# A load of 28 rows split in 26 and 2, and an early store that waits for the landing of the 26

## The chip, the cores and the metric

The kernel runs on one core of a Trainium2 chip. The metric is the time of one execution on the device in microseconds (us). A second execution of the same program is recorded by the hardware profiler; its span runs from the first to the last instruction of the program.

## The reference

There are 16 x 1024 = 16384 tokens, each with 512 float32 values in `x` and 8 router logits. For each token the two largest probabilities of the softmax over the 8 logits are taken and divided by their sum. The output holds the token's 512 values twice, once multiplied by each of the two weights:

```python
probs = np.exp(router_logits - logits_max)
probs = probs / np.sum(probs, axis=-1, keepdims=True)
topk_indices = np.argsort(probs, axis=-1)[..., -k:]          # k = 2
topk_probs = np.take_along_axis(probs, topk_indices, axis=-1)
topk_probs = topk_probs / np.sum(topk_probs, axis=-1, keepdims=True)
x_expanded = x[:, :, np.newaxis, :].repeat(k, axis=2)
return (x_expanded * topk_probs[..., np.newaxis]).astype(np.float32)
```

By the profile the kernel reads 34.08 MB from HBM and writes 67.11 MB.

## The kernel before

The tokens are laid over the 128 partitions, 128 for each partition, in two groups (`GROUPS`): 65 tokens a partition, then 63. In what follows a "row" is one token of each partition: a row of input is 128 x 2 KB = 256 KB, a row of output 512 KB. Tokens of one partition lie side by side in HBM, so that a load or store of n rows moves one contiguous piece a partition.

There are two large buffers. `xs` has room for 65 rows of input. `osp` has room for 18 rows of output; before that it serves as room for the logits and for the steps that find the two largest (`room`). The output of a row is either written into `osp` or, where the input rows have been used up, over input rows in `xs` itself (two rows of `xs` hold one row of output).

**Loads** (`LOADS`, the loop of line 119, issued at line 122). The first group comes in four loads of 2, 4, 28 and 31 rows, the second in three of 16, 16 and 31. All are issued by SyncE, in the order in which they are written. Behind the first 6 rows stand the two loads of the logits (lines 130 and 131), and `top2_weights` is built there: VectorE finds the largest and the second of the 8 logits by maxima and minima, and ScalarE makes the two weights from their difference by two sigmoids (lines 37 and 38), into `WA`.

**Products and stores** (`STORES`, the loop of line 134). One entry is the first row, the number of rows, the buffer, and the place in it. For each entry VectorE makes one product (line 138) of the input rows, each read twice, by the weights; where it is written over a part of `osp` that an earlier store may still be reading, the product is made in two, so that the first rows (`FREE`: 3 and 2) don't wait for the second store to be done. Then the entry is stored (line 151). In the first group the entries are 3, 15, 16, 15 and 16 rows; in the second 16, 16, 15 and 16.

**Queues.** Every load and store is issued by SyncE, in the written order, save one: the first store of the first group, of 3 rows (the early store), which ScalarE issues behind its two sigmoids. The profile shows SyncE's DMAs as queue q1 and ScalarE's as q10. The instructions wait on semaphores for what they need, and SyncE's issues stand in a row: one that waits holds those behind it. The second group's loads are written over the rows of `xs` whose stores they wait for.

Of the kernel before, what the change touches and what calls it, by code (L numbers as in the profile page):

```python
# [1 line left out]

# [4 lines left out]

F32 = mybir.dt.float32
ALU = mybir.AluOpType
ACTF = mybir.ActivationFunctionType  # L10
P = 128


def top2_weights(nc, WA, dlt, room, logits, E):

    tt = nc.vector.tensor_tensor
    hi, lo, n = None, None, E  # L20
    while n > 1:
        n //= 2
        if hi is None:
            a, b = logits[:, :, 0:n], logits[:, :, n : 2 * n]
            nhi, nlo = room(n), b
            tt(nhi, a, b, op=ALU.max)  # L26
            tt(nlo, a, b, op=ALU.min)  # L27
        else:
            a, b = hi[:, :, 0:n], hi[:, :, n : 2 * n]
            nhi, nlo, tmp = room(n), room(n), room(n)  # L30
            tt(tmp, lo[:, :, 0:n], lo[:, :, n : 2 * n], op=ALU.max)  # L31
            tt(nlo, a, b, op=ALU.min)  # L32
            tt(nlo, nlo, tmp, op=ALU.max)  # L33
            tt(nhi, a, b, op=ALU.max)  # L34
        hi, lo = nhi, nlo
    tt(dlt, hi[:, :, 0], lo[:, :, 0], op=ALU.subtract)  # L36
    nc.scalar.activation(WA[:, :, 0], dlt, ACTF.Sigmoid, scale=-1.0)  # L37
    return nc.scalar.activation(WA[:, :, 1], dlt, ACTF.Sigmoid, scale=1.0)  # L38

GROUPS = [65, 63]

LOADS = [[2, 4, 28, 31], [16, 16, 31]]
BASE = [0, 1]

STORES = [
    [(0, 3, "osp", 0), (3, 15, "osp", 3), (18, 16, "xs", 0), (34, 15, "osp", 0), (49, 16, "xs", 33)],
    [(0, 16, "osp", 2), (16, 16, "xs", 0), (32, 15, "osp", 0), (47, 16, "xs", 32)],
]  # L50

L = 18

FREE = [3, 2]


@with_exitstack
def kernel(
    ctx: ExitStack,
    tc: tile.TileContext,  # L60
    x: bass.AP,
    router_logits: bass.AP,
    k: bass.AP,
    out: bass.AP,
):
    nc = tc.nc
    B, S, D = x.shape
    E = router_logits.shape[-1]
    N = B * S
    assert int(k) == 2 and E == 8 and N == P * sum(GROUPS)  # L70
    M = N // P

    x_v, o_v, rl_v = [], [], []
    t0 = 0
    for n in GROUPS:
        t1 = t0 + P * n
        x_v.append(
            x.rearrange("b s d -> (b s) d")[t0:t1].rearrange("(p m) d -> p m d", p=P)
        )
        o_v.append(  # L80
            out.rearrange("b s k d -> (b s) k d")[t0:t1].rearrange(
                "(p m) k d -> p m k d", p=P
            )
        )
        rl_v.append(
            router_logits.rearrange("b s e -> (b s) e")[t0:t1].rearrange(
                "(p m) e -> p m e", p=P
            )
        )
        t0 = t1  # L90

    wpool = ctx.enter_context(tc.tile_pool(name="wpool", bufs=1))
    xs = wpool.tile([P, max(GROUPS), D], F32)
    osp = wpool.tile([P, L, 2, D], F32)
    WA = wpool.tile([P, M, 2], F32)
    dlt = wpool.tile([P, M], F32)


    flat = osp.rearrange("p l k d -> p (l k d)")
    taken = [0]  # L100

    def room(n):
        o = taken[0]
        taken[0] += M * n
        return flat[:, o : o + M * n].rearrange("p (m n) -> p m n", n=n)

    logits = room(E)

    def place(where, at, n):

        if where == "osp":
            return osp[:, at : at + n]
        return xs[:, at : at + 2 * n, :].rearrange("p (r k) d -> p r k d", k=2)

    moved = []
    m0 = 0
    for g, G in enumerate(GROUPS):
        x0, r = BASE[g], 0
        for n in LOADS[g]:
            moved.append(  # L120
                tc.keep_in_program_order(
                    nc.sync.dma_start(  # L122
                        xs[:, x0 + r : x0 + r + n, :], x_v[g][:, r : r + n, :]
                    )
                )
            )
            r += n
            if g == 0 and r == 6:
                n0 = GROUPS[0]
                tc.keep_in_program_order(nc.sync.dma_start(logits[:, :n0], rl_v[0]))  # L130
                tc.keep_in_program_order(nc.sync.dma_start(logits[:, n0:], rl_v[1]))  # L131
                weights = top2_weights(nc, WA, dlt, room, logits, E)
        assert r == G
        for r, n, where, at in STORES[g]:
            og = place(where, at, n)
            again = where == "osp" and at == 0 and r > 0
            for a, b in [(0, FREE[g]), (FREE[g], n)] if again else [(0, n)]:
                product = nc.vector.tensor_tensor(  # L138
                    og[:, a:b],
                    xs[:, x0 + r + a : x0 + r + b, :]  # L140
                    .unsqueeze(2)
                    .to_broadcast([P, b - a, 2, D]),
                    WA[:, m0 + r + a : m0 + r + b, :]
                    .unsqueeze(3)
                    .to_broadcast([P, b - a, 2, D]),
                    op=ALU.mult,
                )

            queue = nc.scalar if g == r == 0 else nc.sync
            moved.append(  # L150
                tc.keep_in_program_order(queue.dma_start(o_v[g][:, r : r + n], og))  # L151
            )
        m0 += G

    seen = tc.keep_in_program_order(nc.sync.nop())
    for ins in [weights, product] + moved[:-1]:
        tc.add_manual_dep(
            seen.ins,
            ins.ins.name,
            mybir.DependencyInfo(  # L160
                mybir.DependencyClass.Sync, mybir.DependencyReason.DATA
            ),
            reason="all but the last transfer is done",
        )


# [1 line left out]
_INS = ['x', 'router_logits', 'k']  # L168
_OUTS = [((16, 1024, 2, 512), 'float32')]

_NUMBERS = {'k': 2}


# [26 lines left out]
```

## Time and profile before

| | |
|---|---|
| time, median of 3 runs | 239.78 us (239.72 to 239.96) |
| the profiled execution | 241.36 us |
| its span | 239.6 us |
| VectorE busy | 141.9 us, 59% of the span, 22 instructions |
| ScalarE busy | 1.8 us |
| read from HBM, written to HBM | 34.08 MB, 67.11 MB; 422 GB/s over the span |
| VectorE's longest waits | for loads of `xs` 47.3 us, 2 times; for stores of `osp` 14.8 us, 2 times |

A profile line that has a count like "x22" gives the number of instructions. SPq and ACTq are the instruction queues of SyncE and ScalarE, where DMAs are issued; the duration beside a DMA issue is that of the issue alone, and the time to its landing is told apart. Times in the timeline are from the start of the span. In windows, the DMA share is the time of all packets that start in the window, over 16 DMA engines; in a narrow window it can be over 1, since a packet is counted whole in the window where it starts.

### The profile page before, as it was taken

To read this page: it belongs to the slowest core of one execution; us is meant where nothing else is said; L and a number is where in the kernel's file an instruction comes from. 1 tells how busy PE (TensorE), PEld (TensorE's weight loads), DVE (VectorE), ACT (ScalarE), POOL (GpSimd) and SP (SyncE) were. 2 spreads that over 40 slices of the span, in tenths; PEclk is the share of its full clock that TensorE was granted. 3 is DMA by queue.
4 is the path that set the end of the run, shared out by engine and by line. 5 is a ranking of instruction groups with operands and counts; after the bars stand their busy time and mean duration, and the time that the engine had idled before them with its cause. 6 is when DMAs were issued, how large, how long until landed. Compare 5 with 4: busy or idle time off the path is not lost.

```text
span 239.6 us, 106 instructions
## 1 busy us (share of the span) xinstructions
DVE 141.9 (59%) x22; ACT 1.8 (1%) x3; POOL 0.2 (0%) x4
## 2 busy tenths in 40 slices
DVE  0560499999789999200000699999405999960000
ACT  2000000000000000000000000000000000000000
POOL 0000000000000000000000000000000000000000
DMA  7989998979989897999899999999999899898984
GB/s 253 528 373 483 427 415 376 493 339 492 481 372 492 383 482 339 482 437 449 361 421 438 438 438 498 435 419 471 405 405 471 372 503 442 380 492 360 514 350 186
DMA packets 2592, 101.19 MB, mean 422 GB/s; under 512 B 288, under 2 KB 416, under 8 KB 672
## 3 DMA queue, kind: packets, MB, share of 16 engines
q1 hardware_dynamic: 2448, 99.62, 96.7%
q10 hardware_dynamic: 144, 1.57, 1.5%
HBM read 34.08 MB, written 67.11 MB: 422 GB/s over the span
## 4 chain that ended last, share of the span: by engine, by line
DMA 48%; DVE 40%; SPq 1%; issue 0%; DVEq 0%
DMA xs<-in_x_dram 25%; DVE osp L138 25%; DMA out_dram<-osp 23%; DVE xs L138 14%; SPq L122 0%; SPq L131 0%; SPq L130 0%; SPq L151 0%; DVEq L138 0%
## 5 line engine op out<-in xcount | busy, mean ns | idle before, releaser
L138 DVE TENSOR_TENSOR osp<-xs,WA 128x3072 f32<-128x3072 f32 (+5 forms) x7 | 69.4, 9909 | 62.7 <-DMA xs<-in_x_dram 47.3
L138 DVE TENSOR_TENSOR xs<-xs,WA 128x16384 f32<-128x16384 f32 x4 | 68.9, 17224 | 0.1
L26 DVE TENSOR_TENSOR osp<-osp 128x512 f32<-128x512 f32 x1 | 0.7, 693 | 8.5 <-DMA osp<-in_router_logits_dram 8.5
L37 ACT ACT_TABLE_LOAD x1 | 1.3, 1283 | 0.7 <-PEq L181 0.7
L27 DVE TENSOR_TENSOR osp<-osp 128x512 f32<-128x512 f32 x1 | 0.7, 691 | 0.0
L32 DVE TENSOR_TENSOR osp<-osp 128x256 f32<-128x256 f32 (+1 forms) x2 | 0.7, 351 | 0.0
L31 DVE TENSOR_TENSOR osp<-osp 128x256 f32<-128x256 f32 (+1 forms) x2 | 0.7, 350 | 0.0
L34 DVE TENSOR_TENSOR osp<-osp 128x256 f32<-128x256 f32 (+1 forms) x2 | 0.7, 350 | 0.0
L33 DVE TENSOR_TENSOR osp<-osp 128x256 f32<-128x256 f32 (+1 forms) x2 | 0.7, 350 | 0.0
L37 ACT ACTIVATE WA<-dlt 128x128 f32<-128x128 f32 x1 | 0.3, 315 | 10.5 <-DVE dlt L36 10.5
L36 DVE TENSOR_TENSOR dlt<-osp 128x128 f32<-128x128 f32 x1 | 0.3, 292 | 0.0
L38 ACT ACTIVATE WA<-dlt 128x128 f32<-128x128 f32 x1 | 0.3, 297 | 0.0
L181 POOL MEMSET const-bfloat16-1.0<- 128x1 bf16 x1 | 0.1, 101 | 0.0
L181 POOL MEMSET const-uint8-127<- 128x1 uint8 x1 | 0.1, 101 | 0.0
L181 POOL MEMSET const-float32-0.0<- 128x1 f32 x1 | 0.1, 98 | 0.2 <-issue 0.2
L181 POOL MEMSET const-float32-1.0<- 128x1 f32 x1 | 0.1, 98 | 0.0
## 6 DMA issues: line engine op xcount, KB each, us to landing
out_dram<-osp SPq DMA_DIRECT2D x3, 7680.0 KB, 23.5
xs<-in_x_dram SPq DMA_DIRECT2D x2, 7936.0 KB, 42.2
xs<-in_x_dram SPq DMA_DIRECT2D x2, 4096.0 KB, 40.1
xs<-in_x_dram SPq DMA_DIRECT2D x1, 7168.0 KB, 24.8
out_dram<-osp ACTq DMA_DIRECT2D x1, 1536.0 KB, 26.6
xs<-in_x_dram SPq DMA_DIRECT2D x1, 1024.0 KB, 5.9
xs<-in_x_dram SPq DMA_DIRECT2D x1, 512.0 KB, 3.9
osp<-in_router_logits_dram SPq DMA_DIRECT2D x1, 260.0 KB, 6.2
```

The source lines that it names most:

```text
L26: tt(nhi, a, b, op=ALU.max)
L27: tt(nlo, a, b, op=ALU.min)
L31: tt(tmp, lo[:, :, 0:n], lo[:, :, n : 2 * n], op=ALU.max)
L32: tt(nlo, a, b, op=ALU.min)
L33: tt(nlo, nlo, tmp, op=ALU.max)
L34: tt(nhi, a, b, op=ALU.max)
L36: tt(dlt, hi[:, :, 0], lo[:, :, 0], op=ALU.subtract)
L37: nc.scalar.activation(WA[:, :, 0], dlt, ACTF.Sigmoid, scale=-1.0)
L38: return nc.scalar.activation(WA[:, :, 1], dlt, ACTF.Sigmoid, scale=1.0)
L138: product = nc.vector.tensor_tensor(og[:, a:b], xs[:, x0 + r + a : x0 + r + b, :] .unsqueeze(2) .to_broadcast([P, b - a, 2, D]), WA[:, m0 ...
L181: nc = _bacc.Bacc("TRN2", target_bir_lowering=False, num_devices=1)
```

## The change

The first group's load of 28 rows is issued as two, of 26 rows and of 2 rows, one behind the other on SyncE; the load of 31 rows follows as before. The early store of three rows, on ScalarE, gets one more thing to wait for: the landing of the load of 26. The second product (rows 3 to 17) then reads rows of the loads of 4 and 26 alone, so that it waits for the load of 26, and the third (rows 18 to 33) waits for the load of 2 as well. The function that adds such waits, `behind`, is also used for the instruction at the end that waits for all but the last transfer, as the code before it did in place. The order of the instructions on every engine is otherwise the same.

```diff
-LOADS = [[2, 4, 28, 31], [16, 16, 31]]
+LOADS = [[2, 4, 26, 2, 31], [16, 16, 31]]
...
+    def behind(ins, others, reason):
+
+        for other in others:
+            tc.add_manual_dep(
+                ins.ins,
+                other.ins.name,
+                mybir.DependencyInfo(
+                    mybir.DependencyClass.Sync, mybir.DependencyReason.DATA
+                ),
+                reason=reason,
+            )
+
...
             r += n
+            if g == 0 and r == 32:
+                landed = moved[-1]
             if g == 0 and r == 6:
...
             queue = nc.scalar if g == r == 0 else nc.sync
-            moved.append(
-                tc.keep_in_program_order(queue.dma_start(o_v[g][:, r : r + n], og))
-            )
+            store = tc.keep_in_program_order(queue.dma_start(o_v[g][:, r : r + n], og))
+            if queue is nc.scalar:
+                behind(store, [landed], "the store goes beside the last load of the group")
+            moved.append(store)
...
     seen = tc.keep_in_program_order(nc.sync.nop())
-    for ins in [weights, product] + moved[:-1]:
-        tc.add_manual_dep(
...
+    behind(
+        seen, [weights, product] + moved[:-1], "all but the last transfer is done"
+    )
```

More of the change, by code (lines that the diff above doesn't have):

```diff
@@ L149 @@
             queue = nc.scalar if g == r == 0 else nc.sync
-            moved.append(
-                tc.keep_in_program_order(queue.dma_start(o_v[g][:, r : r + n], og))
-            )
+            store = tc.keep_in_program_order(queue.dma_start(o_v[g][:, r : r + n], og))
+            if queue is nc.scalar:
+                behind(store, [landed], "the store goes beside the last load of the group")
+            moved.append(store)
         m0 += G
     seen = tc.keep_in_program_order(nc.sync.nop())
-    for ins in [weights, product] + moved[:-1]:
-        tc.add_manual_dep(
[L158 to L164, printed above, removed]
+    behind(
+        seen, [weights, product] + moved[:-1], "all but the last transfer is done"
+    )
 _INS = ['x', 'router_logits', 'k']
```

## The prediction

> **What bounds the kernel now.** I read the page first: the busy shares, the slices and the queues.
>
> ```profile
> span 239.6 us, 106 instructions
> DVE 141.9 (59%) x22; ACT 1.8 (1%) x3; POOL 0.2 (0%) x4
> DMA  7989998979989897999899999999999899898984
> q1 hardware_dynamic: 2448, 99.62, 96.7%
> q10 hardware_dynamic: 144, 1.57, 1.5%
> ```
>
> VectorE works 59% of the span; the packets of the two DMA queues (q1 is SyncE's, q10 is ScalarE's, which carries the early store alone) fill 96.7 + 1.5 = 98.2% of what 16 DMA engines have. The page's chain of waits gives DVE 40% of the span, but a chain through an engine that was released by a DMA doesn't say that the DMA engines stood still meanwhile. So next the stretches: DMA share and GB/s are the last two columns.
>
> ```profile
> 2.00:44.00 42.00, 23.73 (x14) 0.52 (x3) 0.00 (x0) 1.00 1.02 430
> 44.00:124.00 80.00, 50.28 (x4) 0.00 (x0) 0.00 (x0) 1.00 1.00 432
> 124.00:160.00 36.00, 26.38 (x2) 0.00 (x0) 0.00 (x0) 1.00 1.00 431
> 160.00:236.00 76.00, 41.52 (x4) 0.00 (x0) 0.00 (x0) 1.00 1.00 434
> ```
>
> Here the share is 1.00 in every stretch (1.02 in the first, since a packet is counted whole where it starts). The DMA engines go from packet to packet without a hole from 2 to 236 us. The bytes don't change, so only two things can move the time: a hole that the change opens, or packets that take longer or shorter. All holes of before together (1.8% of 239.6 = 4.3 us) lie at the start, before the first packets, and at the end, and the change touches neither.
>
> **Does a hole open?** The timeline of the first group, and the landings of the loads of 7168 KB (28 rows) and 7936 KB (31 rows), issued between 3 and 4 us by the rows of their issues:
>
> ```profile
> 16.40 0.37 ACTq L151 DMA_DIRECT2D out_dram<-osp  x1
> 27.42 16.16 DVE L138 TENSOR_TENSOR osp<-xs,WA 128x15360 f32<-128x15360 f32 x1 [11.04 <-DMA xs<-in_x_dram]
> 43.60 0.35 SPq L151 DMA_DIRECT2D out_dram<-osp  x1
> 43.61 17.22 DVE L138 TENSOR_TENSOR xs<-xs,WA 128x16384 f32<-128x16384 f32 x1
> 60.75 3.35 DVE L138 TENSOR_TENSOR osp<-xs,WA 128x3072 f32<-128x3072 f32 x1
> 60.86 0.34 SPq L151 DMA_DIRECT2D out_dram<-xs  x1
> 67.08 12.96 DVE L138 TENSOR_TENSOR osp<-xs,WA 128x12288 f32<-128x12288 f32 x1 [2.98 <-DMA out_dram<-osp]
> 80.07 0.33 SPq L151 DMA_DIRECT2D out_dram<-osp  x1
> ...
> xs<-in_x_dram SPq DMA_DIRECT2D x1, 7936.0 KB, 45.6
> xs<-in_x_dram SPq DMA_DIRECT2D x1, 7168.0 KB, 24.8
> ...
> out_dram<-xs SPq DMA_DIRECT2D x1, 25.5
> ```
>
> The load of 28 lands at 27.4 (issue near 2.6 + 24.8), and the second product starts then. The load of 31 lands at about 3.3 + 45.6 = 48.9, the second store is issued at 43.60: it stands in the queue 5.3 us before its turn. The third store is issued at 60.86, while the second lands just before 67.08 (the product of 12 rows waits for it and starts then): 6.2 us early. The fourth is issued at 80.07 and the third lands at 60.86 + 25.5 = 86.4: 6.3 us early. VectorE is thus ahead of the queue by 5 us or more at each of these steps, and a product that starts earlier only makes its store stand longer in the queue.
>
> **The packets.** To price the edits I went down to single rounds. A load of 28 rows is 128 packets, one for each partition, 8 on each DMA engine; a window that holds one round has 16 of them, and share times width is the mean packet. The windows of one round each, and then the two queues of 20.0 to 21.3, of 22.9 to 23.95 and of 29.1 to 30.3 (packets, MB, share):
>
> ```profile
> 9.30:10.20 0.90, 0.90 (x2) 0.00 (x0) 0.00 (x0) 1.00 2.35 1019
> 42.30:43.40 1.10, 1.10 (x1) 0.00 (x0) 0.00 (x0) 1.00 2.13 923
> 44.70:45.75 1.05, 1.05 (x1) 0.00 (x0) 0.00 (x0) 1.00 2.44 967
> 131.80:133.00 1.20, 0.00 (x0) 0.00 (x0) 0.00 (x0) 1.00 1.02 437
> 157.90:159.20 1.30, 1.30 (x1) 0.00 (x0) 0.00 (x0) 1.00 1.87 781
> ...
> q1 hardware_dynamic: 16, 0.92, 167.6%
> q10 hardware_dynamic: 14, 0.17, 31.0%
> ...
> q1 hardware_dynamic: 16, 0.92, 241.3%
> q10 hardware_dynamic: 5, 0.06, 13.7%
> ...
> q1 hardware_dynamic: 16, 1.02, 195.2%
> q10 hardware_dynamic: 7, 0.09, 16.8%
> ```
>
> An undisturbed packet of 28 rows takes 2.35 x 0.90 = 2.12 us, one of 31 rows 2.13 x 1.10 = 2.34, so 0.075 a row. A packet of the early store takes 0.168 x 1.2 x 16 / 7 = 0.46. Beside the store, packets of 31 rows still take 1.952 x 1.2 = 2.34: the mixing itself costs nothing. But three rounds are longer. The seventh of the load of 28, where the store comes in, takes 1.676 x 1.3 = 2.18 (+0.06). The eighth and last takes 2.413 x 1.05 = 2.53 (+0.42). The last round of the load of 31, with the second store behind it, takes 2.44 x 1.05 = 2.56 (+0.22). The last round of the second group's load of 31, also with a store behind it, takes 1.87 x 1.30 = 2.43 (+0.09). The second group's load of 16, which has a load behind it, takes 1.02 x 1.20 = 1.22 in its last round, against 2.34 - 15 x 0.075 = 1.21: no stretch. So what I read is this: the last packets of a load stretch where a store is beside or behind them.
>
> The end is set by the engine that is latest. These rows are the last packet of three of those rounds (windows 23.85 to 23.95, 45.6 to 45.75, 159.1 to 159.2), and the packets that start between 235 and 239:
>
> ```profile
> q1 hardware_dynamic: 1, 0.06, 167.5%
> q1 hardware_dynamic: 1, 0.06, 119.9%
> q1 hardware_dynamic: 1, 0.06, 201.6%
> ...
> q1 hardware_dynamic: 17, 0.07, 4.0%
> ```
>
> They take 1.675 x 0.1 x 16 = 2.68 us (+0.56), 1.199 x 0.15 x 16 = 2.88 (+0.54) and 2.016 x 0.1 x 16 = 3.23 (+0.88). After 235 us only one packet with data starts (0.07 MB; the other 16 are completions): one engine is over a round's start behind all others, and its delays count in full. That it is the same engine in all three rows is inferred from its being last each time.
>
> **The change, part by part.**
>
> *The wait of the early store.* ScalarE has nothing queued behind that issue, so nobody else waits on ScalarE. The load of 26 would land at 27.4, less 8 packets by 2 x 0.075 = 1.2, less three packets of the store on the last engine (3 x 0.46 = 1.4, at two packets 0.9), less the stretch (0.56 + 0.06): 24.2. The store is issued then, not at 16.40; in before its packets appear in the 20.0 to 21.3 window, about 3.6 us after the issue, so they come at about 28, into the second round of the load of 31. Its 8 rounds by 2.34 + 0.46 = 2.8 end near 50, and the next to need its room is the product of three rows, at 24.2 + 16.2 + 17.2 = 57.6. Cover 7 us; if the last two packets alternate with those of the second store (2 x 2.3) it is still 3.
>
> *The earlier second product*: 24.2, not 27.4, and so the second store's issue at 40.4, not 43.6, the third's at 57.6, not 60.9. Both then stand 3.2 us longer in the queue. The product of 12 rows waits for the second store's landing at 67 as before, and from there all is as before. Value: 0. A hole would need the load of 31 to end over 8 us early.
>
> *The split.* One more issue on SyncE, 0.35 to 0.4 us by the issue rows, ahead of the load of 31 (queued some 20 us before its turn): 0. On each engine 8 packets of 26 rows and 8 of 2 rows take the place of 8 of 28. The line through 28 and 31 rows gives 2.12 - 28 x 0.075 = 0.02 for a packet without rows, and 1.22 - 16 x 0.075 = 0.02 comes out for 16 rows, completions included; rounded down, an additional packet costs 0.01: 8 x 0.01 = +0.08, at most twice that.
>
> *The stretch.* The last round of the load of 26 has the load of 2 behind it and no store in flight: by the load of 16 no stretch, -0.56 - 0.06 on the last engine, -0.48 on the mean. The store now comes in during the load of 31: +0.06 to +0.1. The last round of the load of 31 then has the store beside it and another behind it; each of the two alone gave +0.54 to +0.56 on the last engine, so I leave it as it is, but for the other engines it goes from +0.22 to +0.42. The sum for the last engine is -0.62 + 0.08 + 0.08 = -0.46, for a mean engine -0.48 + 0.20 + 0.08 + 0.08 = -0.12. How far the last engine's lag follows the mean I can't tell from one execution, so I take a value between them: -0.33. Bounds of the unshown (the stretch in its new place): -1.0, if the last round of 31 also loses its 0.54; +0.64, if nothing is saved and it carries both prices (0.56 + 0.08).
>
> The profiled execution took 241.36 us about a span of 239.6; the three plain times have the median 239.78 and I carry the difference over to it: 239.78 - 0.33 = 239.45 us. A difference within 0.2% (0.48 us) is about what a measurement of this kernel can't tell from none.
>
> **A rule that speaks against it.** The Trainium skill, DMA: Bandwidth & Descriptors, section Anatomy of one DMA, puts a fixed cost of about 2.0 us on every DMA (it says so of those issued from GpSimd), and its section Bandwidth advises at least 1 MiB a transfer; the new load of 2 rows has half of that. By that page, were the cost on the path, the sum would be near 241.5. No run here has the split yet; the rows by which I judge it come next.
>
> **The rivals.**
>
> 1. *The stretch moves with the store* (0.28). The price belongs to the store's entry, not to the end of the load: it is paid in the first rounds after entry, now those of the load of 31. For it: the two stretched rounds are also the two next to the entry. Against: the load of 31 stretches in its last round too, with no new queue. It gives 239.78 + 0.08 = 239.85.
>
> 2. *Both prices meet* (0.13), slower: the last round of the load of 31 carries that of the store beside it and that of the store behind it, and the entry still costs what it did. Against: the second group's last round has +0.09 on the mean. It gives up to 239.78 + 0.64 = 240.4, and decides from where the last engine's packet there takes over 2.34 + 1.0.
>
> 3. *The last engine catches up* (0.10): the second store now is queued some 8 us ahead of its turn, as in the second group, where the mean round grew by only 0.09; then the last round of 31 loses its 0.54 as well: 239.78 - 1.0 = 238.8.
>
> 4. *Each DMA costs its latency on the queue* (0.03), slower. The price by rows:
>
> ```profile
> 0.72 0.37 SPq L122
> 1.15 0.42 SPq L122
> ...
> xs<-in_x_dram SPq DMA_DIRECT2D x1, 1024.0 KB, 5.9
> xs<-in_x_dram SPq DMA_DIRECT2D x1, 512.0 KB, 3.9
> ```
>
> The first load of 2 rows lands 3.9 us after its issue, of which 8 x (0.02 + 2 x 0.075) = 1.4 are packets: 2.5 remain, 242.3. Against it: the load of 4 rows lands at 7.05, 2.4 us after that of 2 rows (4.6), and 8 x 4 x 0.075 = 2.4 are its packets alone. Successive loads follow each other without the latency.
>
> That the change doesn't do what it says can't be: the store is ready 8 us before the landing it now waits for.
>
> **How the numbers follow.** My forecast has 0.46. Of it, a third lies below 239.30 (faster by over 0.2%). Rival 1 lies within, rival 3 below, rival 2 mostly above 240.26, rival 4 above. Faster 0.15 + 0.10 = 0.25; slower 0.13 + 0.03 and a little of rival 1: 0.17; the same 0.58. The range leaves out rival 4, the deepest part of rival 3 and the top of rival 2: 239.0 to 240.3.
>
> **What would show it.** Right: the product of 15 rows starts near 24.2, the second store is issued near 40.4, the share stays 1.00, the last round of the load of 26 takes 1.97, and the early store's first packets come near 28. Wrong: a stretch with a share under 1.00 (a hole), the rounds after the store's entry longer by 0.4 (rival 1), the last packet of the load of 31 over 3.3 us (rival 2), a gap of microseconds between the landings of the loads of 26 and of 2 beyond 1.4 (rival 4).

## The result, and the profile after

| | before | after |
|---|---|---|
| time, median | 239.78 us, later 239.87 to 239.97 | 241.6 us (241.31 to 242.03, 6 runs) |
| ratio after to before | | 1.0072 [1.0057, 1.0087] |
| the profiled execution | 241.36 us | 241.73 us |
| its span | 239.6 us | 240.0 us |

The change makes the kernel slower by about 1.8 us, where the forecast was 0.33 us faster and the range ended at 240.3. Spans of the two profiles hardly differ, because the profiled execution of before was itself 1.6 us above its median; a second one of the same kernel, shown below as the first experiment, took 239.87 us with a span of 238.1, and I compare with that.

The page after, in parts (span and queues):

```profile
span 240.0 us, 109 instructions
q1 hardware_dynamic: 2592, 99.62, 96.9%
q10 hardware_dynamic: 144, 1.57, 1.5%
```

The 144 packets more on q1 are those of the load of 2 rows: 128 with data and 16 completions. The stretches after (DMA share and GB/s last):

```profile
2.00:44.00 42.00, 27.08 (x14) 0.52 (x3) 0.00 (x0) 1.00 1.05 445
44.00:124.00 80.00, 46.93 (x4) 0.00 (x0) 0.00 (x0) 1.00 0.99 423
124.00:160.00 36.00, 26.48 (x2) 0.00 (x0) 0.00 (x0) 1.00 1.02 432
160.00:236.00 76.00, 41.41 (x4) 0.00 (x0) 0.00 (x0) 1.00 1.00 434
```

The share stays about 1.00 everywhere: no hole opened. The rate, though, is higher in the first stretch (445 against 430 GB/s), and lower in the second (423 against 432). Part of this is the edge of the window: the last round of the load of 31, 1.02 MB, starts before 44 us here and behind it in the kernel before. So the landings have to say where the time goes. The timeline of the first group after, and the time to landing of the load of 2 rows, of the early store and of the fourth:

```profile
24.07 16.16 DVE L152 TENSOR_TENSOR osp<-xs,WA 128x15360 f32<-128x15360 f32 x1 [7.85 <-DMA xs<-in_x_dram]
24.14 0.37 ACTq L164 DMA_DIRECT2D out_dram<-osp  x1
40.25 0.35 SPq L164 DMA_DIRECT2D out_dram<-osp  x1
57.51 0.34 SPq L164 DMA_DIRECT2D out_dram<-xs  x1
65.85 12.96 DVE L152 TENSOR_TENSOR osp<-xs,WA 128x12288 f32<-128x12288 f32 x1 [5.10 <-DMA out_dram<-osp]
78.83 0.33 SPq L164 DMA_DIRECT2D out_dram<-osp  x1
...
xs<-in_x_dram SPq DMA_DIRECT2D x1, 512.0 KB, 22.1
...
out_dram<-osp ACTq DMA_DIRECT2D x1, 1536.0 KB, 25.9
...
out_dram<-osp SPq DMA_DIRECT2D x1, 7680.0 KB, 24.4
```

Up to the fourth store the instructions start about as the prediction has it, ahead of before. The fourth store is issued at 78.83 and lands 24.4 us later, at 103.2; in the second profile of before (its rows stand under the first experiment) it is 79.18 + 24.4 = 103.6. At 103 us the changed kernel is 0.35 us early. At the end it is 1.9 us late by the spans. So the loss lies between 103 us and the end, where the change touches no instruction.

I found it by the prediction's own means, single rounds: a window that holds the 16 packets of one round, share times width being the mean packet. Of after, the last round of the load of 26, the last round of the fifth store (16 rows of `xs`, with the second group's first load behind it), and the last round of the second group's load of 31 (with a store behind it):

```profile
21.00:21.80 0.80, 0.00 (x0) 0.00 (x0) 0.00 (x0) 1.00 2.46 1065
119.00:120.70 1.70, 0.00 (x0) 0.00 (x0) 0.00 (x0) 1.00 1.75 617
157.60:159.40 1.80, 1.80 (x1) 0.00 (x0) 0.00 (x0) 1.00 1.74 564
```

The first is undisturbed: 2.46 x 0.80 = 1.97 us. The second takes 1.75 x 1.70 = 2.98 and the third 1.74 x 1.80 = 3.13. Undisturbed, they are 2.42 (the same window of before below, 1.42 x 1.70, gives it but for the rounding of the share) and 2.34 (the prediction's packet of 31 rows). These two rounds are 0.56 and 0.79 us too long on the mean engine, 1.35 together. Both places are turns of SyncE's queue, at 119 us from stores to loads and at 158 from loads to stores, and so is the end of the load of 31 near 45 us; I call what such a round takes beyond its undisturbed length its excess.

### The profile page after: what moved, and what is told of

Same layout as the page of the kernel before. It is cut to its first block, busy times and chain, and to the rows that moved or that the text cites. A ratio compares the mean times of both kernels' runs of the same rounds, so it can differ in the third digit from the quotient of the medians.

```text
span 240.0 us, 109 instructions
## 1 busy us (share of the span) xinstructions
DVE 141.9 (59%) x22; ACT 1.8 (1%) x3; POOL 0.2 (0%) x4
## 4 chain that ended last, share of the span: by engine, by line
DMA 48%; DVE 40%; SPq 1%; issue 0%; DVEq 0%
DVE osp L152 25%; DMA xs<-in_x_dram 24%; DMA out_dram<-osp 24%; DVE xs L152 14%; SPq L134 0%; SPq L145 0%; SPq L144 0%; SPq L164 0%; DVEq L152 0%
## 6 DMA issues: line engine op xcount, KB each, us to landing
out_dram<-osp SPq DMA_DIRECT2D x3, 7680.0 KB, 24.4
out_dram<-osp ACTq DMA_DIRECT2D x1, 1536.0 KB, 25.9
```

## The experiments

The time of each run is set beside the median of the runs of before on the same chip: 239.97 us for the first four, 239.94 for the fifth to the eighth, 239.91 for the ninth to the twelfth, 239.87 for the last six. The last columns are the mean engine's excess in us, worked out as above (packets of the early store in such a window taken off at 0.46 us each): of the rounds before 50 us that are too long by 0.1 us or more, of the round at 119, and of that at 158. The ratio is not that of the two medians; its interval tells how far the executions of both kernels scatter.

| kernel | median us | ratio | early | 119 | 158 |
|---|---|---|---|---|---|
| before again | 240.1 | 1.0004 [0.9991, 1.0017] | 0.42 | 0 | 0.09 |
| split only | 240.64 | 1.0026 [1.0011, 1.0040] | 1.12 | 0 | 0.05 |
| wait only | 241.5 | 1.0057 [1.0041, 1.0074] | 0.27 | 0.30 | 0.88 |
| after again | 241.6 | 1.0065 [1.0046, 1.0083] | 0.15 | 0.37 | 0.74 |
| one queue | 240.21 | 1.0013 [1.0004, 1.0022] | 0.97 | 0 | 0.07 |
| after, filler that came too early | 241.26 | 1.0058 [1.0042, 1.0073] | 0.23 | 0.37 | 0.95 |
| store ends in the loads | 240.0 | 1.0024 [0.9992, 1.0057] | 0.58 | 0 | 0.13 |
| early store beside the second | 241.59 | 1.0066 [1.0051, 1.0082] | 0 | 0.81 | 0.77 |
| second store waits for early | 243.22 | 1.0120 [1.0093, 1.0147] | 0.23 | 0.78 | 0.98 |
| after, real filler | 241.26 | 1.0055 [1.0030, 1.0079] | 0.30 | 0.35 | 0.99 |
| after, load of 31 split | 239.75 | 0.9993 [0.9977, 1.0009] | 0.37 | 0.01 | 0.18 |
| two store queues | 239.97 | 0.9991 [0.9974, 1.0008] | 0.39 | 0 | 0.04 |
| boundary before the store's run | 246.17 | 1.0262 [1.0244, 1.0279] | 0.68 | 0.71 | 0.76 |
| boundary at its end | 240.25 | 1.0016 [1.0000, 1.0031] | 0.53 | 0 | 0.11 |
| one queue, store between loads | 240.97 | 1.0055 [1.0033, 1.0078] | 1.21 | 0 | 0.15 |
| early store in two, early and late | 240.22 | 1.0014 [0.9998, 1.0031] | 0.78 | 0 | 0.04 |
| boundary before the run, products ordered | 240.22 | 1.0019 [1.0006, 1.0032] | 0.71 | 0 | 0.09 |
| load of 31 split, products ordered | 239.82 | 0.9994 [0.9984, 1.0004] | 0.34 | 0 | 0.05 |

**The two halves of the change.** First the kernel before, unchanged; then each part alone; then the changed kernel again.

> The kernel before, unchanged, for a second profile: its first profiled execution took 241.36 us where the plain times have 239.78, so it was not typical. Theory 1 (the long last packets of loads are what makes an execution long): an execution near 239.8 shows the last packets of the second group's load of 31 at about 2.34 us on all engines, the last engine too (3.23 in the first profile), and ends some 1.5 us earlier. Theory 2 (the difference is outside the span): the same packets, the same span of 239.6, and a shorter total.

Its page, the issue of its fourth store, and the two late rounds:

```profile
span 238.1 us, 106 instructions
q1 hardware_dynamic: 2448, 99.62, 97.2%
...
79.18 0.33 SPq L151 DMA_DIRECT2D out_dram<-osp  x1
...
119.00:120.70 1.70, 0.00 (x0) 0.00 (x0) 0.00 (x0) 1.00 1.42 617
157.60:159.40 1.80, 1.80 (x1) 0.00 (x0) 0.00 (x0) 1.00 1.35 564
```

The rounds take 2.41 and 2.43 us: nothing at 119 and 0.09 at 158. Its only excess of 0.1 us or more is early, in the last round of the load of 28. The packets of both queues fill 97.2 + 1.5 = 98.7% of 238.1 us, 235.0 us on the mean engine; after, 98.4% of 240.0, 236.2 us. So 1.2 of the 1.9 us between the spans are longer packets of the mean engine. The other 0.7 is about the lag of the latest engine: the last 16 packets with data start within 0.67 us of each other here (233.9 to 234.6), and within 1.76 us after (234.7 to 236.4), where the latest starts 1.31 us behind their mean and not 0.45.

The split alone (on before):

```diff
-LOADS = [[2, 4, 28, 31], [16, 16, 31]]
+LOADS = [[2, 4, 26, 2, 31], [16, 16, 31]]
```

> The load of 28 is split in 26 and 2, the early store does not wait. If the split is what costs (its additional packets, or what they shift later): +1.2 to +1.8 us over before. If the wait is what costs: +0.1 us (8 more packets an engine by about 0.01 us each).

It costs 0.67 us against its own before. The last round of its load of 26, which has the early store beside it, and the late round at 158:

```profile
21.50:22.20 0.70, 0.00 (x0) 0.00 (x0) 0.00 (x0) 1.00 4.49 1252
157.60:159.40 1.80, 1.80 (x1) 0.00 (x0) 0.00 (x0) 1.00 1.33 564
```

4.49 x 0.70 = 3.14 us is for 16 packets of 26 rows and two of the early store; less 2 x 0.46 / 16 that is 3.09, where 1.97 is undisturbed: +1.12. The price is all early, and 158 has 0.05 (2.39).

The wait alone (the load of 28 whole, the early store waits for it):

```diff
+            if g == 0 and r == 34:
+                landed = moved[-1]
...
+                behind(store, [landed], "the store goes beside the last load of the group")
```

> The load of 28 stays whole and the early store waits for its landing (about 25.3 us). If the wait, that is the store's place beside the load of 31, is what costs: +1.2 to +1.8 us. If the split costs: no change, or -0.4 by the stretch that the load of 28 loses.

It costs 1.53 us, and its rounds (last of the load of 28, then 119 and 158) show where:

```profile
22.00:22.80 0.80, 0.00 (x0) 0.00 (x0) 0.00 (x0) 1.00 2.65 1147
119.00:120.70 1.70, 0.00 (x0) 0.00 (x0) 0.00 (x0) 1.00 1.60 617
157.60:159.40 1.80, 1.80 (x1) 0.00 (x0) 0.00 (x0) 1.00 1.79 564
```

Early, the load of 28 is undisturbed (2.65 x 0.80 = 2.12). Late, 2.72 and 3.22. With the wait alone the early price falls from 0.42 to 0.27, and a larger one stands at the two late turns.

The changed kernel again:

> The changed kernel, unchanged, on the same chip, for a second profile: 241.6 us again. If the long packets near 119 to 123 us and near 158 us (together about +1 us on the mean engine) belong to the change, they are there again; if they come by chance, they are elsewhere or gone.

It gave 241.6 us once more, with +0.37 and +0.74 at the two turns. So the late price isn't an accident of one profile. The parts don't add: 0.67 + 1.53 = 2.2, together 1.6 to 1.8, since with the wait the split no longer pays its early price.

**Two queues, or the store's place?** The early store on SyncE, behind the loads (on before):

```diff
-            queue = nc.scalar if g == r == 0 else nc.sync
+            queue = nc.sync
```

> The kernel before, with the early store issued by SyncE behind the load of 31 instead of by ScalarE: no second queue, no mixing of packets, the store's bytes follow the load of 31. Theory M (the early store's mixing with the load's end makes the packets near 23 us long, and where it ends beside the second store it makes those near 120 and 158 us long): no long packets anywhere but a little at 48 us, 239.2 to 239.5 us. Theory L (the second product and so the second and third store come 2 to 3 us earlier; that lead is what makes the late packets long): the packets near 120 and 158 us are long, 241 to 241.5 us.

0.27 us slower, between the two expectations, and the price is early, in the last round of the load of 31:

```profile
40.40:41.20 0.80, 0.80 (x1) 0.00 (x0) 0.00 (x0) 1.00 4.14 1270
119.00:120.70 1.70, 0.00 (x0) 0.00 (x0) 0.00 (x0) 1.00 1.42 617
```

4.14 x 0.80 = 3.31 against 2.34, and nothing at 119. The Trainium skill (DMA: Bandwidth & Descriptors, Issuing engines are not separate DMA queues) says that starting DMAs from several engines saves only the time of issuing. For queue against queue this run nearly agrees (0.27 us). But the early store on the same ScalarE queue, issued at the landing of the load of 28 (25.3) and not at 16.4, cost 1.5 us in the run of the wait alone: what counts here is when it enters, of which that section tells nothing.

Does a later store of its own on ScalarE's queue cost anything by itself? The fourth store put there (on before):

```diff
+            queue = nc.scalar if g == 0 and r in (0, 34) else nc.sync
```

> The kernel before, with the fourth store (15 rows, issued near 80 us) on ScalarE's queue instead of SyncE's, so that it runs beside the third and the fifth store. Theory M in its general form (two queues that store at once leave the later changes between loads and stores dear): long packets near 120 and 158 us, 241 us or more. If only the early store's place matters: 239.9 to 240.2 us.

It is no slower, with 0 and 0.04 at the turns. So a second queue that carries a store is not in itself what costs.

**Is it VectorE's lead, or an early store that reaches the second?** In the changed kernel the second store is issued 3 us sooner (40.25), and the early store's last packets come close to the second store's first. To take the lead away, three rows of the second product are made twice:

```diff
+            if g == 0 and r == 3:
+                parts = [(0, 3)] + parts
```

> The changed kernel with the first three rows of the second product made twice (3.36 us more on VectorE), so that the second and third store are issued at about 43.6 and 60.9 us as in the kernel before. Theory L (lead of the stores): the late long packets go, about 240.2 us. Theory M (where the early store lies among the packets): 241.6 us as the changed kernel.

The experiment missed its aim. The row of the added product, in the timeline:

```profile
12.88 6.62 DVE L155 TENSOR_TENSOR osp<-xs,WA 128x3072 f32<-128x3072 f32 x2 [0.58 <-ACT WA L38]
```

The added rows need only the loads of 2 and 4, so they were made at 12.88, ahead of the wait, and the second store still went at 40.32. It counts as another run of the changed kernel (241.26). With the last three rows instead, which come with the load of 26, the filler works (timeline, then the two late rounds):

```diff
+                parts = parts + [(n - 3, n)]
```

> The changed kernel with the last three rows of the second product made again behind it (3.4 us more on VectorE, this time behind the wait for the load of 26, so that it does delay): the second and third store are issued near 43.6 and 61 us as in the kernel before. Theory L (the lead of the stores): late long packets gone, about 240.2. Theory M: 241.6, late long packets as in the changed kernel.

```profile
43.67 0.35 SPq L167 DMA_DIRECT2D out_dram<-osp  x1
119.00:120.70 1.70, 0.00 (x0) 0.00 (x0) 0.00 (x0) 1.00 1.63 617
157.60:159.40 1.80, 1.80 (x1) 0.00 (x0) 0.00 (x0) 1.00 1.85 564
```

The second store is issued at 43.67, as in the kernel before, and the price stays (2.77 and 3.33 us). The lead isn't the cause.

The early store brought to an end within the loads (the wait alone, with the load of 31 in two):

```diff
+LOADS = [[2, 4, 28, 16, 15], [16, 16, 31]]
```

> The early store waits for the landing of the load of 28 (whole), and the load of 31 is split in 16 and 15 rows, so that its 8 packets an engine run beside 8 shorter load packets and end before the last load does. Theory M: with the store's end among loads there are no long packets near 120 and 158 us, 240.0 to 240.7 us. Theory L, and theory W (any store that enters after the landing of the 28 does it): 241.5 us or more.

The late price is gone (0 and 0.13; the second is this row) and 0.58 is paid early:

```profile
157.60:159.40 1.80, 1.80 (x1) 0.00 (x0) 0.00 (x0) 1.00 1.37 564
```

The median is 240.0 us, but the interval of its ratio reaches from 0.9992 to 1.0057. Now the opposite, the early store let in only when the second product is done (load of 28 whole):

```diff
+            if g == 0 and r == 3:
+                store = tc.keep_in_program_order(nc.scalar.dma_start(*early))
+                behind(store, [product], "the store goes beside the second store")
```

> The early store is issued once the second product is done (near 41.5 us), so that nearly all its packets run beside the second store's. Theory M (ending beside a store is what counts): long packets near 120 and 158 us as in the changed kernel or longer, 241.3 us or more. If it is the mixing with loads alone that counts: as one queue, 239.2 to 239.6 us.

241.59 us, nothing early, and the largest excess at 119 of all:

```profile
119.00:120.70 1.70, 0.00 (x0) 0.00 (x0) 0.00 (x0) 1.00 1.90 617
157.60:159.40 1.80, 1.80 (x1) 0.00 (x0) 0.00 (x0) 1.00 1.73 564
```

Both fitted the theory that the early store running up to or beside the second is the trigger. So that was taken away by itself: the changed kernel, with its second store waiting for the landing of the early one.

```diff
+            if g == 0 and r == 3:
+                behind(store, [early], "the second store follows the early one")
```

> The changed kernel, but the second store also waits for the landing of the early store (near 50 us): the two never run beside each other. That opens a hole of 3 to 5 us at the DMA engines near 48 to 52 us. Theory M (an early store that still runs beside the second store makes the packets near 120 and 158 us long): those late packets are short again, so the time is 241.6 + hole - 1.3, and the sum of the late long packets (1.3 to 1.4 us on the mean engine in the changed kernel) is under 0.3. If the place beside the last load is what counts: they stay long, 241.6 + hole.

```profile
48.02 0.35 SPq L164 DMA_DIRECT2D out_dram<-osp  x1
...
46.00:48.00 2.00, 2.00 (x1) 0.00 (x0) 0.00 (x0) 1.00 0.47 197
121.00:123.00 2.00, 0.00 (x0) 0.00 (x0) 0.00 (x0) 1.00 1.60 524
160.00:162.00 2.00, 2.00 (x1) 0.00 (x0) 0.00 (x0) 1.00 1.66 508
```

The second store goes at 48.02 and never runs beside the early one, and both late rounds are long all the same (3.20 and 3.32). That speaks against the theory, but the wait also opened a hole (share 0.47 from 46 to 48), and everything behind came about 2 us later, so this run doesn't settle it; the early store in two, below, does.

**A turn within the loads.** The changed kernel with its load of 31 in two:

```diff
+LOADS = [[2, 4, 26, 2, 16, 15], [16, 16, 31]]
```

> The changed kernel with the load of 31 split in 16 and 15, so that the early store's 8 packets an engine end among loads. Theory M: no late long packets, 239.5 to 240.2 us; if the split of the 28 is what counts besides: 241 or more.

```profile
157.60:159.40 1.80, 1.80 (x1) 0.00 (x0) 0.00 (x0) 1.00 1.40 564
```

The late price is gone (0.01 and 0.18), and 239.75 is level with before. Is it that a boundary of loads falls within or behind the early store's run? Two other places for it:

```diff
+LOADS = [[2, 4, 26, 2, 4, 27], [16, 16, 31]]
```

> The changed kernel with the load of 31 split in 4 and 27 rows: the boundary between these two lies near 27.5 us, before or just as the early store's first packets come. Theory B (a boundary of loads within the early store's run is what spares the late packets): late packets long, near 241.5 us. If the mere splitting of the load spares them: 240 us.

```diff
+LOADS = [[2, 4, 26, 2, 27, 4], [16, 16, 31]]
```

> The changed kernel with the load of 31 split in 27 and 4 rows: the boundary lies at the end of the early store's run, whose last packets may run beside the load of 4. Theory B: late packets short, near 240 us. If the boundary has to lie early in the run, or the early price has to be paid before 40 us: late packets long, near 241.5.

The second is as expected of a harmless boundary (240.25; 0.53 early, 0.11 late). The first was at 246.17, not by the boundary but by the scheduler that orders the instructions when the program is built. It put a product of three rows ahead of one of 16, and VectorE waited:

```profile
48.84 3.36 DVE L152 TENSOR_TENSOR osp<-xs,WA 128x3072 f32<-128x3072 f32 x1 [8.60 <-DMA out_dram<-osp]
...
64.00:70.00 6.00, 6.00 (x2) 0.00 (x0) 0.00 (x0) 1.00 0.03 10
124.00:125.70 1.70, 0.00 (x0) 0.00 (x0) 0.00 (x0) 1.00 1.84 617
163.50:165.50 2.00, 2.00 (x1) 0.00 (x0) 0.00 (x0) 1.00 1.55 508
```

The third store came late and the DMA engines stood still from 64 to 70 (share 0.03). It had paid 0.68 early, and behind the hole it paid 0.71 and 0.76 again. The same order came about in the two runs with the load of 31 in 16 and 15 rows; there VectorE waited under 2 us and no hole opened, but the third store was issued near 63 us and not near 58. With the products held in the written order, the same loads:

```diff
-                product = nc.vector.tensor_tensor(
+                product = tc.keep_in_program_order(nc.vector.tensor_tensor(
```

> The changed kernel with the load of 31 split in 4 and 27 rows, and VectorE's products kept in the written order (without that the product of three rows came ahead of that of 16 and waited). The boundary lies before the early store's packets come. Theory B: no hole, late packets near 120 and 158 us long (1.2 us or more on the mean engine), 241.3 to 241.9 us. If any split of the load of 31 spares them: 239.7 to 240.3.

```profile
44.10:44.90 0.80, 0.80 (x1) 0.00 (x0) 0.00 (x0) 1.00 3.66 1198
119.00:120.70 1.70, 0.00 (x0) 0.00 (x0) 0.00 (x0) 1.00 1.42 617
157.60:159.40 1.80, 1.80 (x1) 0.00 (x0) 0.00 (x0) 1.00 1.35 564
```

240.22, the price early (0.71; the first row is the last round of the load of 27, 2.93 us with six packets of the early store in it, 2.76 without them, where an undisturbed one has 27 x 0.075 + 0.02 = 2.04) and 0.09 late. So where the boundary lies doesn't decide. The load of 31 split in 16 and 15, with the products held likewise:

> The changed kernel with the load of 31 split in 16 and 15 rows and the products kept in the written order, so that the third store is issued near 57.5 us and not 62.7. Theory B: late packets short as before; the third store's issue has cover, so the time is that of the same split without the order, 239.6 to 239.9 us.

239.82, with 0.34 early and 0.05 late: the order of the products isn't what spared the late price. The best versions are level with before, and none beats it.

**Is a late place of the early store harmful by itself?** The store stays on one queue, but stands between the loads of 28 and 31 (on before):

```diff
+        for n in LOADS[g] if g else LOADS[g][:-1]:
+            load(n)
...
+            if g == r == 0:
+                r = 34
+                load(31)
```

> One queue: SyncE issues the early store between the loads of 28 and 31, no mixing. Theory P: the change from load to store and back near 25 us is where a price of 0.4 to 1.0 us is paid, and the late packets are short: 239.8 to 240.3 us. Theory B (needs the second queue): late packets long, 241 or more; no price anywhere: 239.3.

1.1 us slower, more than theory P had, and the price is early: 1.00 in the last round of the load of 28 and 0.21 in that of the load of 31, against 0.15 late. Its profiled execution took 242.2 us, 1.2 above the median of this version. And the early store in two on ScalarE, one row at once, two rows when the load of 28 has landed:

```diff
-    [(0, 3, "osp", 0), ...
+    [(0, 1, "osp", 0), (1, 2, "osp", 1), ...
```

> The early store in two: one row is stored at once as in the kernel before (it runs across the end of the load of 28), two rows wait for the landing of the 28 as in the run with the wait alone. Theory P (the early price spares the late one): late packets short, 240.0 to 240.4 us. Theory T (a store that lies late is what harms): late packets long, 241.3 us or more.

```profile
42.30:43.50 1.20, 1.20 (x1) 0.00 (x0) 0.00 (x0) 1.00 2.83 942
157.60:159.40 1.80, 1.80 (x1) 0.00 (x0) 0.00 (x0) 1.00 1.32 564
```

Two of the three rows wait for the same landing as in the wait alone, and nothing is paid at 158; instead the last round of the load of 31 takes 2.83 x 1.20 = 3.40 with 14 packets of the store (0.11 MB by 8 KB), 3.12 without them. A late place by itself doesn't bring the late price. Nor does running beside the second store: the second store's first packets start at 46.2, and these are the two queues from 47.3 to 57:

```profile
q1 hardware_dynamic: 63, 3.87, 92.0%
q10 hardware_dynamic: 63, 0.42, 10.2%
```

0.42 MB of the early store (some 51 packets by 8 KB) run among the packets of the second store, and the late price is not there.

**What stands.** Of the 18 runs and the two profiles shown first, those that paid 0.34 us or more before 50 us paid 0.19 or less at the two late turns together; those that paid 0.30 or less paid 1.1 to 1.8 there. One run breaks the rule, the one with the hole from 64 to 70, which paid on both sides of it. That the late price comes and goes with the early one is shown by six edits that brought an early price back and took the late one away (the load of 31 split on the wait alone, on the changed kernel, and there with products ordered; the boundary behind 27 rows, and behind 4 with products ordered; the store in two). Whether the early price spares the late one, or both follow from a third thing, is not shown, and what carries it from 45 us to 119 in the DMA engines is not settled. How far apart the engines run doesn't decide: in the kernel after the 16 packets of the round at 119 start within 0.41 us of each other, in the run whose early store ends in the loads within 0.37, and only the first pays. The size of the early price can't be the whole of it, since 0.30 (the real filler) and 0.34 (the load of 31 split, ordered) lie side by side with opposite outcomes.

## Why the prediction was wrong

**What held.** The second product was to start near 24.2 (24.07), the second store to be issued near 40.4 (40.25), the third near 57.6 (57.51), the share to stay at 1.00 (0.99 to 1.05). The early store's first packets, expected near 28, come at 29.1. The last round of the load of 26 takes 1.97 as forecast. The early store lands at 24.14 + 25.9 = 50.0, "near 50", and the rounds beside it kept their length. SyncE's queue from 43.3 to 44.2 of after, the last round of the load of 31:

```profile
q1 hardware_dynamic: 16, 1.02, 267.8%
```

It takes 2.678 x 0.9 = 2.41, only +0.07 on the mean where +0.42 was written. By 103 us a gain was there, 0.35 us. That this is nearly the 0.33 of the forecast is luck: 0.33 was chosen between two sums worked out from an execution that was not typical. The gain is about the 0.42 of the load of 28, less the 0.08 for the packets of the split.

**The step that failed** stands in the part on the earlier second product: "from there all is as before. Value: 0." For the earlier product itself the 0 held: with the lead taken away by the real filler the late price stayed. But no part of the sum, that on the wait of the early store included, has a term for anything behind 67 us. That was argued from the order of the instructions and from the lead of VectorE, and both are as it says. But the packets of the same instructions took 0.56 and 0.79 us longer at 119 and 158 us. The prediction had the row for this kind of price in hand: three rounds that stretch at a turn of the queue. It took each turn's price as belonging to what stands beside or behind the load there, so that a price removed in one place was saved for good. In the runs, where the early one goes, larger ones stand at the later turns: the wait alone, with 0.27 early, has 0.30 and 0.88 there and costs 1.53 us. The split was mis-sized too: +0.08 in the sum, +0.67 us measured alone, though beside the wait this early price is not paid.

**A second step**: the saving was weighed on the last engine of one profiled execution (+0.56, +0.54, +0.88 for its long packets). That execution took 241.36 us, 1.6 above the median, and in the second profile of before no packet with data starts after 235 us. Windows 235 to 236 and 236 to 237, first of that profile, then of after:

```profile
235.00:236.00 1.00, 0.00 (x0) 0.00 (x0) 0.00 (x0) 1.00 0.00 0
...
235.00:236.00 1.00, 0.00 (x0) 0.00 (x0) 0.00 (x0) 1.00 0.76 328
236.00:237.00 1.00, 0.00 (x0) 0.00 (x0) 0.00 (x0) 1.00 0.15 66
```

The lag priced there was that execution's own. In a typical one only the 0.42 of the load of 28 could be saved. The prediction carried the difference over to the median, though the saving was drawn from just what set that execution apart.

**The rivals.** The price that moves to the first rounds after entry (1): no, those rounds are undisturbed. Both prices at the load of 31 (2): it alone had the right sign at a fair chance, but its place was wrong (only +0.07 there, while the price stands at the later turns). The last engine that catches up (3): the load of 31 has almost no stretch after, but it has none in the second profile of before either (2.35 us), so nothing was caught up there. A latency for each DMA on the queue (4) came nearest of the rivals in the number, 242.3, and is wrong: the load of 2 lands 1.27 us after that of 26 (its product starts at 24.07; the load of 2 is issued at 3.2 and takes 22.1), of which 8 x 0.17 = 1.4 would be its packets alone. The rule beside it, the 2.0 us fixed cost of the Trainium skill (DMA: Bandwidth & Descriptors, Anatomy of one DMA), would have given 241.5, next to the 241.6 measured, but that is luck. It doesn't apply to queued loads here: the version with the loads of 26, 2, 16 and 15, two DMAs more than before, took 239.82 us against 239.87.

## What to carry to other kernels

In a kernel whose DMA engines are busy without a hole, price an edit over the whole queue, not to the point where the instructions fall back into step: look at the last round before each turn between loads and stores, to the end of the kernel. Take a second profile before weighing anything on the last packets of the slowest engine. And measure the parts of a change alone: here the wait cost 1.5 us and the split 0.7, and the two together were not their sum.

## What the runs showed of the hardware that was not expected

At a turn of the queue the last round of a DMA took up to 1.0 us longer on the mean engine than an undisturbed one (0.99 at 158 us with the real filler), and up to 1.1 where the early store ran beside the end of a load (3.09 for 1.97, the split alone). Whether it did at 119 and 158 us went with what had happened before 50 us, by instructions that had long been done. A sign of it can be read on SyncE. The longest issue of a load of `xs` (these are the first two loads of the second group, issued between 96 and 102 us) took 1.21 to 1.25 us in all runs that paid late, and at most 1.10 in the others. The issues of the loads in the kernel after and then in the one with the boundary behind 4 rows and products ordered (min, median and max in ns):

```profile
L134 SPq DMA_DIRECT2D xs<-in_x_dram x8: 328/478/1242, 0.7 to 123.1; - x8
...
L134 SPq DMA_DIRECT2D xs<-in_x_dram x9: 328/439/821, 0.7 to 123.6; - x9
```

Whether that issue's length is a cause or only shows the same state of the engines was not tried.
